# A transformer block on TensorE: the big SBUF buffers moved to other addresses

## The chip, the cores and the metric

The kernel runs on one core of one Trainium2 chip. The metric is the device time of one execution in microseconds, here the median of three runs.

## What is computed

One layer of a hybrid block on 256 tokens with 16 meta tokens ahead of them (272 in all), of width 2048, in float32: a feed-forward block, a mixer (windowed pooling beside latent attention, gated and projected), and a second feed-forward block, each with a norm before and after.

```python
def _swiglu(h, w_gu, w_down):
    g, u = jnp.split(h @ w_gu, 2, axis=-1)
    return (jax.nn.silu(g) * u) @ w_down

def _hybrid_mixer(h, w_in, ...):
    z = h @ w_in
    u_pool, c_q, c_kv, k_rope, g_pool, g_mla = jnp.split(z, SPLITS, axis=-1)
    y_pool = _multiscale_pool(u_pool, pool_w, pool_scale) @ w_pool_o
    y_mla = _mla(c_q, c_kv, k_rope, q_a_norm, w_q_b, kv_a_norm, w_kv_b, cos, sin) @ w_mla_o
    y = jax.nn.sigmoid(g_pool) * y_pool + jax.nn.sigmoid(g_mla) * y_mla
    return y @ w_out

h = h + 0.5 * _rmsnorm(_swiglu(_rmsnorm(h, norm_ffn1_pre[i]), ffn1_w_gu[i], ffn1_w_down[i]), norm_ffn1_post[i])
m = _hybrid_mixer(_rmsnorm(h, norm_mix_pre[i]), ...)
h = h + _rmsnorm(m, norm_mix_post[i])
h = h + 0.5 * _rmsnorm(_swiglu(_rmsnorm(h, norm_ffn2_pre[i]), ffn2_w_gu[i], ffn2_w_down[i]), norm_ffn2_post[i])
return h[:, N_META:]
```

The feed-forward blocks are 5632 wide, the attention has 16 heads.

## The kernel before

All activations stay in SBUF, transposed: features on the 128 partitions, tokens along the row. The weights come as one long stream of 128x128 tiles in the order of their use. A chunk of 8 tiles is loaded by one DMA on SyncE's queue into one of five `raw` buffers (4096 bytes in each partition), well ahead of its use. Four tiles at a time are split into two parts of 12 bits, `hi` (ScalarE, L92) and `lo` (VectorE, L93), in the type fp32r; each has six buffers of 2048 bytes. A product is then the sum of high by high, high by low and low by high.

The activations that are multiplied are split in the same way by the class `Two`, which keeps the high and the low part of a tile side by side. The weights' tile is always the stationary operand, the tokens are the moving one. There are two ways to issue the product with one tile of weights:

- `mm3` (L213 to L215), the narrow way: three matmuls, of 272 columns where all tokens take part and of 256 where the meta tokens don't. The first and the second load the high part of the weights, the third the low part. Their moving operands are the high, the low and again the high part of the tokens.
- `mm_wide` (L219 and L221): one matmul of 512 columns, the high part of the weights by both parts of 256 tokens, and one of 256 columns, the low part by the high one.

The first feed-forward and the first part of the mixer's `w_in` (up to about 920 us) are narrow with 272 columns. The gates (the rest of `w_in`, about 930 to 1115 us) are wide, but their moving operand `x` is laid out for 272 tokens, so that the 256 tokens begin 64 bytes into each row of 1088 bytes. The attention (to about 1300 us) has short products of many kinds: q, k, v, scores, probabilities by values, and the pooled branch's output projection `po`. From then on everything is wide, with operands laid out for 256 tokens: `o` by `w_mla_o` (to about 1400 us), `y` by `w_out`, and `x` and `a` in the second feed-forward. There a tile of the moving operand takes 2048 bytes, high part and low part of 1024 each. In the layout for 272 tokens it takes 2176, 1088 each.

Nothing is issued by a planner: the order is the program's own, with small delays counted in tiles of weights (`later`). The pools of SBUF lie one behind the other in the order in which they are opened, each buffer rounded up to 32 bytes:

- `keep`: `gains` (448 bytes), `const` (1024: identity and ones), `eps` (8), `acc`, `rs` (1088 each) and `small` (64);
- `raw`: five buffers; `parts`: six of `hi`, then six of `lo`;
- `big`: nine slots of 17408 bytes (34 times 512). They hold the residual `h`, the moving operands `x`, `a`, `y`, `o`, `D`, `Y`, `CB`, and other large tensors (`t`, `zp`, `zm`, `U`, `MA`, `VP`), each in turn;
- `tmp`: six buffers of 1088 bytes for single tiles on their way from PSUM, and some small ones.

Of the kernel before, what the change touches and what calls it, by code (L numbers as in the profile page):

```python
# [9 lines left out]
F32 = mybir.dt.float32  # L10
# [4 lines left out]
P = 128  # L15
# [3 lines left out]
R = 256  # L19
# [8 lines left out]
CH, PT = 8, 4  # L28
# [12 lines left out]
class Nothing:  # L41
    """Stands in for the builder's objects while the order of the weights is collected."""

# [16 lines left out]
class Weights:  # L60
    """The weights as one stream of [128, 128] tiles in the order of their use; each chunk of CH
    tiles is loaded ahead, and split, PT tiles at a time, into two parts of 12 bits, which together
    are the float32."""

# [32 lines left out]
    def take(self, *tiles):  # L97
        """The next tiles of the stream, side by side."""
        n = len(tiles)
        room = PT - len(self.order) % PT  # L100
        if room < n:
            self.order += [None] * room
        at = len(self.order)
        self.order += tiles
        if self.plan is None:
            return Nothing(), Nothing()
        assert self.plan[at : at + n] == list(tiles)
        p, j = divmod(at, PT)
        self.load((p + HL - 1) * PT // CH + RAW)
        self.divide(p + min(HL - 1, p // 2 + 2))  # L110
        for _ in tiles:
            self.tick()
        hi, lo = self.split[p]
        s = slice(j * P, (j + n) * P)
        return hi[:, s], lo[:, s]


class Later:
    """Work that is issued some steps of the weights' stream later, so that an engine isn't held
    by what another one has yet to do."""  # L120

# [3 lines left out]
    def __call__(self, *steps):  # L125
        """steps: pairs of a delay after the one before, and what to run then."""
        at = self.now
        for delay, run in steps:
            at += delay
            self.due.append((at, run))  # L130
        self.due.sort(key=lambda d: d[0])
# [11 lines left out]
def build(nc, tc, ctx, hT, wsrc, gains_d, const_d, tables_d, out, order):  # L143
# [6 lines left out]
    raw = ctx.enter_context(tc.tile_pool(name="raw", bufs=RAW))  # L150
    parts = ctx.enter_context(tc.tile_pool(name="parts", bufs=HL))
    big = ctx.enter_context(tc.tile_pool(name="big", bufs=9))
    tmp = ctx.enter_context(tc.tile_pool(name="tmp", bufs=6))
    psum = ctx.enter_context(tc.tile_pool(name="psum", bufs=8, space=bass.MemoryType.PSUM))

    later = Later()
# [14 lines left out]

# [1 line left out]
    h = slot3(KD, L, F32, "h")  # L173
# [9 lines left out]
    ident, ones = const[:, :P], const[:, P:]  # L183
    eps = keep.tile([P, 2], F32, tag="eps", name="eps")
    pool_e.memset(eps[:, 0:1], EPS)
    pool_e.memset(eps[:, 1:2], 4 * EPS)
    acc = keep.tile([P, L], F32, tag="acc", name="acc")
    rs = keep.tile([P, L], F32, tag="rs", name="rs")
    small = keep.tile([P, 16], F32, tag="small", name="small")

# [3 lines left out]
    class Two:  # L194
        """n tiles of T tokens in two parts of 12 bits, side by side."""

# [20 lines left out]
    def mm_wide(b, w, x, k, first, last):  # L217
        """The same with the product of the low part of x in columns of its own, from R on."""
        mm(b.rearrange("p (b c) -> p b c", b=2), w[0], x.both(k, R), start=first, stop=last,  # L219
           skip_group_check=True)  # L220
        mm(b[:, :R], w[1], x.hi(k, R), start=False, stop=last, skip_group_check=True)  # L221

    def join(b, s):
        """s: the sum of both halves of b, in two steps."""
        act(s, b[:, R:], AF.Copy)
        return GAP, lambda: dve.tensor_tensor(s, b[:, :R], s, op=ALU.add)

    def warm(n, x=ident):
        """Keeps the tensor engine's clock up while it has to wait."""
        b = bank("warm")  # L230
        for _ in range(n):
            mm(b[:, :P], x[:, :P], x[:, :P], start=True, stop=True)

# [1 line left out]
    def rms_sums(sources, T, n, half=False):  # L235
        """1 / sqrt(mean + eps), or half of it, of the tokens whose squares' sums over the
        partitions of `sources` add up to n * mean; the tokens are on partitions."""
        b = bank("rms")
        tt = (0, P, L - P)[: 3 if T == L else 2]
        m, c0 = len(tt), 400  # L240
        for i, s in enumerate(sources):
            for j, t0 in enumerate(tt):
                mm(b[:, c0 + j : c0 + j + 1], s[:, t0 : t0 + P], ones[:, :1],
                   start=i == 0 and j == 0, stop=i == len(sources) - 1, skip_group_check=True)
        sd = tmp.tile([P, 4], F32, tag="sd", name="sd", bufs=2)
        f = 4 if half else 1
        act(sd[:, :m], b[:, c0 : c0 + m], AF.Sqrt, scale=f / n, bias=eps[:, f // 4 : f // 4 + 1])
        dve.reciprocal(sd[:, :m], sd[:, :m])
        return b, sd

    def rms_spread(b, sd, T):
        """The same for all partitions, in the bank's first T columns."""
        for j, (t0, c) in enumerate(((0, 0), (P, 0), (L - P, P - NMETA))[: 3 if T == L else 2]):
            mm(b[:, t0 + c : t0 + P], sd[:, j : j + 1].to_broadcast([P, P]), ident[:, c:],
               start=True, stop=True)
# [8 lines left out]
    def squares(src, T, j, last=False):  # L264
        """Adds the squares of src to acc; the last ones stay apart, for `rms` to add."""
        if j == 0:
            act(acc[:, :T], src, AF.Square)
            return []
        s = temp("sq")
        act(s[:, :T], src, AF.Square)  # L270
        if last:
            return [s]
        pool_e.tensor_tensor(acc[:, :T], acc[:, :T], s[:, :T], op=ALU.add)  # L273
        return []
# [3 lines left out]

# [1 line left out]
    class Stream:  # L280
        """The residual stream's parts for the next products; `update` brings a tile of it up to
        date. Issued in stages that lead the products by a tile."""

# [18 lines left out]
        def scale(self):  # L302
            """The pre-norm's scales; products of the unscaled input are scaled by them."""
            b, sd = rms_sums([acc] + self.last, self.T, DM)
# [6 lines left out]
    def products(names, n_k, x, T, wave, evac, stream=None, hooks={}, narrow=()):  # L311
        """Tiles of x @ w, transposed: the first `wave` of them side by side, then one by one."""
        wide = [T == R and i not in narrow for i in range(len(names))]
# [32 lines left out]

# [1 line left out]
    def post(names, n_k, x, T, g_post, half, wave, wait):  # L348
# [26 lines left out]

# [1 line left out]
    def ffn(x, w_gu, w_down, g_post, wait):  # L377
# [27 lines left out]

    # ================= first feed-forward =================
    warm(10, zero)
# [8 lines left out]

    # ================= mixer =================
    x = advance(t, b, L, G_MPRE)
# [15 lines left out]
    def rotate(o, src, T):  # L434
        """Rotary embedding of rows [x1, x2, x1, x2] of 32 each; o may not be src."""
        c = slice(L - T, L)
# [33 lines left out]
    def windows(j):  # L470
        """Difference of the windows' means and the input, in parts."""
        w = WINDOWS[j // 2]
        s = u[:, j, :]
        n, i = 1, 0
# [17 lines left out]

    # columns of w_in in tiles: c_kv, k_rope twice, c_q, u_pool
    names = [("w_in", ("kv", j)) for j in range(4)] + [("w_in", ("kr", 0))]
# [57 lines left out]

# [1 line left out]
    o2 = Two(HEADS, R, "o")  # L554
# [40 lines left out]
    def proj_v(g):  # L595
        """Rows of v of four heads: tokens 0.., tokens 128.., and those from 256 on, by the high
        part of the input in rows 64.. and by the low part in rows 80.. ."""
        bs = [bank(f"v{i}") for i in range(3)]
# [47 lines left out]
    def turn(i):  # L646
        """Transposes the probabilities: keys 128.. and keys 0.. of the two times 128 queries. Of
        the first 128 queries' keys from 128 on only 16 exist, the rows below are zero; the second
        ones' keys from 256 on go to rows 64.. and again to rows 80.. of the last columns."""
        b = bank("pt")  # L650
# [49 lines left out]

# [1 line left out]
    y = Two(KD, R, "y")  # L702
# [17 lines left out]

    # ================= second feed-forward =================
    t, b = ffn(advance(t, b, R, G_F2PRE), "ffn2_w_gu", "ffn2_w_down", G_F2POST, (0, 0))
# [15 lines left out]
def columns(name, m):  # L738
    """Columns of a weight that make its tile m."""
    a = np.arange(P)  # L740
# [71 lines left out]
```

## Time and profile before

| | us |
|---|---|
| median of three runs | 2245.56 (2245.35 to 2246.13) |
| profiled execution, from its first to its last instruction | 2257.5 |
| TensorE busy in it | 2234.3 |
| VectorE, ScalarE, GpSimd busy | 1362.2, 1142.5, 205.4 |

The span is that of one execution under the profiler; no other time of that execution is listed. It is 11.9 us longer than the median of the runs. In the profile, PE is TensorE's matmuls and PEld its weight loads, which overlap them; DVE is VectorE, ACT is ScalarE, POOL is GpSimd, SP is SyncE. A group of the profile reads: line, engine, operation, what it writes and reads, shapes, number; busy time and the mean length of one; idle time of the engine before them and what ended it. Matmuls are pipelined, so the length of a single one is longer than the distance from its start to the next one's start, and that distance is what a matmul costs.

### The profile page before, as it was taken

To read this page: it belongs to the slowest core of one execution; us is meant where nothing else is said; L and a number is where in the kernel's file an instruction comes from. 1 tells how busy PE (TensorE), PEld (TensorE's weight loads), DVE (VectorE), ACT (ScalarE), POOL (GpSimd) and SP (SyncE) were. 2 spreads that over 40 slices of the span, in tenths; PEclk is the share of its full clock that TensorE was granted. 3 is DMA by queue.
4 is the path that set the end of the run, shared out by engine and by line. 5 is a ranking of instruction groups with operands and counts; after the bars stand their busy time and mean duration, and the time that the engine had idled before them with its cause. 6 is when DMAs were issued, how large, how long until landed. Compare 5 with 4: busy or idle time off the path is not lost.

```text
span 2257.5 us, 39449 instructions
## 1 busy us (share of the span) xinstructions
PE 2234.3 (99%) x15040; PEld 2062.4 (91%) x15040; DVE 1362.2 (60%) x2456; ACT 1142.5 (51%) x2273; POOL 205.4 (9%) x229
## 2 busy tenths in 40 slices
PE   9999999999999999999999999999999999999997
PEld 9999999999999999988888888888888888888886
DVE  6555555555444477766666677577666666654554
ACT  6444444444444454555544555665555555554543
POOL 2000000000000053200121111150000000000001
PEclk9999999999999999999999999999999999999999
DMA  6555555555555545566533356545655555655553
GB/s 242 178 175 174 179 172 178 177 170 177 177 169 180 175 150 168 178 190 188 173 113 122 114 169 195 186 151 186 185 188 184 188 186 186 187 191 187 187 182 117
DMA packets 109311, 393.46 MB, mean 174 GB/s; under 512 B 12288, under 2 KB 13696, under 8 KB 109120
## 3 DMA queue, kind: packets, MB, share of 16 engines
q1 hardware_dynamic: 108576, 389.19, 53.7%
q8 instruction: 118, 1.93, 0.4%
q0 software_dynamic: 400, 1.61, 0.2%
q14 instruction: 73, 0.60, 0.1%
q10 hardware_dynamic: 144, 0.13, 0.0%
HBM read 388.78 MB, written 2.10 MB: 173 GB/s over the span
## 4 chain that ended last, share of the span: by engine, by line
PE 97%; DVE 2%; issue 1%; DMA 0%; ACT 0%; SPq 0%; ACTq 0%; DVEq 0%
PE m L219 29%; PE m L221 15%; PE m L213 13%; PE m L215 12%; PE m L214 12%; PE w L219 2%; PE w L214 1%; PE w L221 1%; PE w L215 1%; PE s L622 1%; PE w L213 1%; PE po L213 1%; PE po L215 1%; PE po L214 1%; PE s L621 1%
## 5 line engine op out<-in xcount | busy, mean ns | idle before, releaser
L93 DVE TENSOR_TENSOR lo<-raw,hi 128x512 fp32r<-128x512 f32 x1472 | 1042.9, 722 | 691.7 <-ACT hi L92 686.7
L92 ACT ACTIVATE hi<-raw 128x512 fp32r<-128x512 f32 x1472 | 882.5, 625 | 393.6 <-PE m L214 283.1
L219 PE MATMUL m<-x,hi 128*128 128x512 f32 x1824 | 643.3, 398 | 0.0
L221 PE MATMUL m<-x,lo 128*128 128x256 f32 x1824 | 513.0, 281 | 0.0
L213 PE MATMUL m<-x,hi 128*128 128x272 f32 (+1 forms) x1488 | 429.6, 289 | 0.0
L215 PE MATMUL m<-x,lo 128*128 128x272 f32 (+1 forms) x1488 | 429.2, 288 | 0.0
L214 PE MATMUL m<-x,hi 128*128 128x272 f32 (+1 forms) x1488 | 428.4, 288 | 0.0
L219 PEld LDWEIGHTS m<-x,hi 128*128 128x128 f32 x1824 | 342.9, 188 | 83.2
L221 PEld LDWEIGHTS m<-x,lo 128*128 128x128 f32 x1824 | 345.0, 189 | 0.0
L214 PEld LDWEIGHTS m<-x,hi 128*128 128x128 f32 x1488 | 282.9, 190 | 0.0
L213 PEld LDWEIGHTS m<-x,hi 128*128 128x128 f32 x1488 | 279.8, 188 | 0.0
L215 PEld LDWEIGHTS m<-x,lo 128*128 128x128 f32 x1488 | 279.7, 188 | 0.0
L219 PE MATMUL m<-a,hi 128*128 128x512 f32 x660 | 233.2, 399 | 0.0
L273 POOL TENSOR_TENSOR acc<-acc,sq 128x272 f32<-128x272 f32 (+1 forms) x88 | 83.4, 948 | 1532.8 <-ACT sq L270 1532.5
L215 PE MATMUL m<-a,lo 128*128 128x272 f32 (+1 forms) x748 | 215.7, 288 | 0.0
L213 PE MATMUL m<-a,hi 128*128 128x272 f32 (+1 forms) x748 | 215.7, 288 | 0.0
L214 PE MATMUL m<-a,hi 128*128 128x272 f32 (+1 forms) x748 | 215.3, 288 | 0.0
L221 PE MATMUL m<-a,lo 128*128 128x256 f32 x660 | 185.4, 281 | 0.0
L219 PEld LDWEIGHTS m<-a,hi 128*128 128x128 f32 x660 | 124.1, 188 | 31.1
L214 PEld LDWEIGHTS m<-a,hi 128*128 128x128 f32 x748 | 142.4, 190 | 0.0
L213 PEld LDWEIGHTS m<-a,hi 128*128 128x128 f32 x748 | 140.8, 188 | 0.0
L215 PEld LDWEIGHTS m<-a,lo 128*128 128x128 f32 x748 | 140.8, 188 | 0.0
(206 smaller groups left out, 2577.4 us busy)
## 6 DMA issues: line engine op xcount, KB each, us to landing
raw<-w SPq DMA_DIRECT2D x735, 512.0 KB, 3.5
h<-hT POOLq DMA_DIRECT2D x4, 272.0 KB, 5.7
out<-t SPq DMA_DIRECT2D x8, 128.0 KB, 1.9
out<-t SPq DMA_DIRECT2D x4, 256.0 KB, 2.1
h<-hT SPq DMA_DIRECT2D x1, 544.0 KB, 9.1
raw<-w SPq DMA_DIRECT2D x2, 256.0 KB, 3.5
MA<-tables POOLq DMA_DIRECT2D x1, 480.0 KB, 3.7
h<-hT SPq DMA_DIRECT2D x2, 136.0 KB, 2.9
```

The lines of the kernel that those rows point to most:

```text
L92: nc.scalar.activation(hi, t, AF.Copy)
L93: nc.vector.tensor_tensor(lo, t, hi.bitcast(F32), op=ALU.subtract)
L213: mm(o, wh, xh, start=first, stop=False)
L214: mm(o, wh, xl, start=False, stop=False)
L215: mm(o, wl, xh, start=False, stop=last)
L219: mm(b.rearrange("p (b c) -> p b c", b=2), w[0], x.both(k, R), start=first, stop=last, skip_group_check=True)
L221: mm(b[:, :R], w[1], x.hi(k, R), start=False, stop=last, skip_group_check=True)
L273: pool_e.tensor_tensor(acc[:, :T], acc[:, :T], s[:, :T], op=ALU.add)
L621: mm(b[:, c : c + n], q[:, t0 : t0 + P], k[:, :n], start=True, stop=False)
L622: mm(b[:, c : c + n], qp[hp : hp + 64, t0 : t0 + P], kpe[hp : hp + 64, :n], start=False, stop=True)
```

## The change

`eps` moves from `keep` to a pool of its own, `shift`, with one buffer of 64 bytes that lies between `parts` and `big`. `small` grows from 16 to 80 columns; nothing more is stored in it. With the two, the buffers that follow get other addresses in each partition:

| buffers | before | after | before, modulo 512 | after, modulo 512 |
|---|---|---|---|---|
| `acc`, `rs` | 18016, 19104 | 17984, 19072 | 96, 160 | 64, 128 |
| `raw` (five, every 4096) | 20256 | 20480 | 288 | 0 |
| `hi` (six, every 2048) | 40736 | 40960 | 288 | 0 |
| `lo` (six, every 2048) | 53024 | 53248 | 288 | 0 |
| nine slots of `big` (every 17408) | 65312 | 65600 | 288 | 64 |
| `tmp`, first of six (every 1088) | 221984 | 222272 | 288 | 64 |

Before, all of these are 32 past a multiple of 64; afterwards they are multiples of 64. The difference between a slot's address and that of a weight buffer grows by 64 bytes.

```diff
     parts = ctx.enter_context(tc.tile_pool(name="parts", bufs=HL))
+    shift = ctx.enter_context(tc.tile_pool(name="shift", bufs=1))
     big = ctx.enter_context(tc.tile_pool(name="big", bufs=9))
...
-    eps = keep.tile([P, 2], F32, tag="eps", name="eps")
+    eps = shift.tile([P, 16], F32, tag="eps", name="eps")
     pool_e.memset(eps[:, 0:1], EPS)
     pool_e.memset(eps[:, 1:2], 4 * EPS)
     acc = keep.tile([P, L], F32, tag="acc", name="acc")
     rs = keep.tile([P, L], F32, tag="rs", name="rs")
-    small = keep.tile([P, 16], F32, tag="small", name="small")
+    small = keep.tile([P, 80], F32, tag="small", name="small")
```

The rest of the diff takes out comments. The instructions of every engine and every queue, and their order, are the same before and after; the lines of the program stand one further down from the new pool on (L213 becomes L214, L219 becomes L220).

## The prediction

> **What bounds the kernel now.** I read the summary page first, then the chain of work that ended last, the costliest groups, the list of what TensorE waited for, a table by stretches of time, and last the single matmuls in order of time.
>
> ```profile
> span 2257.5 us, 39449 instructions
> PE 2234.3 (99%) x15040; PEld 2062.4 (91%) x15040; DVE 1362.2 (60%) x2456; ACT 1142.5 (51%) x2273; POOL 205.4 (9%) x229
> PEclk9999999999999999999999999999999999999999
> PE 97%; DVE 2%; issue 1%; DMA 0%; ACT 0%; SPq 0%; ACTq 0%; DVEq 0%
> ...
> L93 DVE TENSOR_TENSOR lo<-raw,hi 128x512 fp32r<-128x512 f32 x1472 | 1042.9, 722 | 691.7 <-ACT hi L92 686.7
> L92 ACT ACTIVATE hi<-raw 128x512 fp32r<-128x512 f32 x1472 | 882.5, 625 | 393.6 <-PE m L214 283.1
> L219 PE MATMUL m<-x,hi 128*128 128x512 f32 x1824 | 643.3, 398 | 0.0
> L221 PE MATMUL m<-x,lo 128*128 128x256 f32 x1824 | 513.0, 281 | 0.0
> L213 PE MATMUL m<-x,hi 128*128 128x272 f32 (+1 forms) x1488 | 429.6, 289 | 0.0
> ...
> L213 PE MATMUL m<-a,hi 128*128 128x272 f32 (+1 forms) x748 | 215.7, 288 | 0.0
> ```
>
> TensorE is busy for 2234.3 of 2257.5 us at the full granted clock, and the chain lies on it for 97%. Its matmuls show no idle time before them. VectorE and ScalarE wait: the first for ScalarE's high parts, the second for TensorE to free a buffer of weights. Nothing shortens this kernel but shorter matmuls, and every nanosecond per matmul tells 15040 times. What TensorE waited for is next to nothing; the largest entry of that list is
>
> ```profile
> PE w L219 <- DVE x L298: 3.6, 7, 0.7
> ```
>
> A busy TensorE is not one at its peak, so I look at how many matmuls go through in a stretch (columns: the stretch, its length, busy time of PE with the number of its matmuls, then weight loads, VectorE, ScalarE, GpSimd, granted clock, DMA share, GB/s).
>
> ```profile
> 300.00:400.00 100.00, 100.00 (x799) 100.00 (x798) 57.38 (x103) 47.57 (x84) 0.00 (x0) 1.00 0.54 174
> 1000.00:1080.00 80.00, 80.00 (x465) 70.33 (x465) 48.73 (x89) 42.82 (x89) 0.56 (x2) 1.00 0.60 189
> 1320.00:1400.00 80.00, 80.00 (x463) 70.61 (x462) 59.36 (x101) 42.71 (x89) 16.22 (x16) 1.00 0.56 183
> 1900.00:2000.00 100.00, 100.00 (x567) 86.71 (x566) 64.72 (x123) 52.69 (x109) 0.00 (x0) 1.00 0.58 180
> ```
>
> I take one off each count, since a stretch cuts a matmul at its edge. In 300 to 400 us (narrow products, three matmuls of 272 columns for each tile of weights, "a triple") a matmul takes 100/798 = 125.3 ns, a triple 376. In 1900 to 2000 (wide products, 512 and 256 columns, "a pair") a pair takes 100/283 = 353.4 ns. In 1320 to 1400 the same two instructions, with `o` as the moving operand, take 80/231 = 346.3 ns. In 1000 to 1080 (the gates) 18 of the matmuls are those of the pooled products, six on each of three lines (by the groups of that stretch,
>
> ```profile
> L215 PE MATMUL pool<-D,lo 128*128 128x256 f32 x6 | 1.7, 281 | 0.0
> ```
>
> ), about 2.1 us at a third of a pair each, so a pair takes (80 - 2.1)/223 = 349.3 ns. So the same work on TensorE costs up to 2% more or less by stage, with the clock the same and no waits.
>
> The single narrow matmuls show that this goes with position, too (start, length, line; L213 begins a triple):
>
> ```profile
> 300.34 0.29 PE L213 MATMUL m<-x,hi 128*128 128x272 f32 x1
> ...
> 300.72 0.29 PE L213 MATMUL m<-x,hi 128*128 128x272 f32 x1
> ...
> 301.09 0.29 PE L213 MATMUL m<-x,hi 128*128 128x272 f32 x1
> ...
> 301.48 0.28 PE L213 MATMUL m<-x,hi 128*128 128x272 f32 x1
> ...
> 301.85 0.29 PE L213 MATMUL m<-x,hi 128*128 128x272 f32 x1
> ...
> 302.23 0.28 PE L213 MATMUL m<-x,hi 128*128 128x272 f32 x1
> ```
>
> From start to start 0.38, 0.37, 0.39, 0.37, 0.38 us: every second triple is about 10 ns dearer. In the program's addresses one thing alternates so: tile k of a narrow moving operand lies 2176 bytes, which is 4 times 512 and 128 more, after tile k-1, while the weight tiles lie 512 bytes apart. So the distance between what streams and what is being loaded, taken modulo 256, takes two values in turn. (The weight tile's own place in its buffer alternates as well, so this is a strong hint and no proof.)
>
> **The change, part by part.**
>
> *The weights' stationary parts `hi`, `lo`, and `raw`, from 288 to 0 modulo 512; the slots from 288 to 64.* On the wide products whose moving operand is laid out for 256 tokens, the moving address less the weight's goes from 0 to 64 modulo 256 in every pair. The nearest rows are the gates': their operand is laid out for 272 tokens and read 64 bytes in, so this distance is 64 and 192 in turn (and the 512 columns are in two pieces). They take 349.3 against 353.4. I take this row, since half of its pairs have exactly the new distance: 353.4 - 349.3 = 4.1 ns less. The pairs concerned are those of the second feed-forward and the output projection:
>
> ```profile
> L219 PE MATMUL m<-x,hi 128*128 128x512 f32 x1824 | 643.3, 398 | 0.0
> L219 PE MATMUL m<-a,hi 128*128 128x512 f32 x660 | 233.2, 399 | 0.0
> L219 PE MATMUL m<-y,hi 128*128 128x512 f32 x144 | 50.9, 399 | 0.0
> ```
>
> The gates' 32 tiles of 16 steps are 512 of the 1824, so 1824 - 512 + 660 + 144 = 2116 remain, and the waves of six tiles that begin the second feed-forward and the output projection add 6 x 16 each: 2308. Times 4.1 ns: 9.5 us less. The gates themselves get the distances 128 and 0 in place of 64 and 192, and the `o` stage leaves its good pattern of 346.3: if both land at 351, that is 512 x 1.7 + 256 x 4.7 = 2.1 us more. Bounds: all pairs as `o` now (2308 x 7.1 = 16 us less), or all one such step of 7.1 ns dearer than now (16 us more).
>
> *The narrow triples.* Their distances are 0 or 128 for the high part and 64 or 192 for the low part now; afterwards it is the other way round. The same four values occur, so I cost this at nothing. Bounds: every triple like the cheap ones (370 against 376: 6 x 2236 = 13 us less, with 1488 + 748 triples from the groups) or like the dear ones (385: 20 us more).
>
> *The attention's short products* (q, k and the pooled output) have all three distances at 0 now and get 64:
>
> ```profile
> L213 PE MATMUL po<-Y,hi 128*128 128x256 f32 x120 | 35.1, 293 | 0.0
> ```
>
> At the pair's saving of 4.1 ns for two matmuls, 2 ns for each is 1.4 us less: the code has 16 heads with 8 + 4 + 2 tiles (a rope tile serves two heads), three matmuls each, 672. Bounds: the same up and down.
>
> *Starts at a multiple of 64.* Every fp32r operand of this kernel starts 32 bytes past a multiple of 64 now, and none will afterwards. No row shows a matmul of this type with an aligned start. I take 0, as in the rows that only change the distance; what it may bring at most is the first rival, and a loss from alignment alone nothing in the trace suggests.
>
> *The operands of the other engines move too.* The 1472 splits take 625 ns on ScalarE and 722 ns on VectorE for four weight tiles; TensorE takes 4 x 376 = 1504 ns for four tiles, or 4 x 353 = 1412. A tenth more or less on either stays hidden. If that cover went, TensorE would show waits for `hi` or `lo`. The same covers the landing of `raw` (DMA share 0.54 to 0.60, the next chunk is five buffers ahead).
>
> *`eps` in a pool of its own, `small` of 80 columns, comments taken out.* No instruction is added or moved on any engine or queue; `eps` is still set twice by GpSimd in the first microseconds. Nothing.
>
> Sum: -9.5 + 2.1 + 0 - 1.4 = -8.8 us: the span of 2257.5 becomes 2248.7. The profiled span is 11.9 us over the median of the runs (2245.56); with the same difference, 2236.8, 0.4% less. Under 0.2% a measurement of this kernel could hardly tell from no change.
>
> **What the Trainium skill would make of it.** Two of its rules speak to the excess. "TensorE: Matmul & The Clock Gate", section Back-to-back issue gap, gives an isolated matmul N/2.4 + 2.5 ns; an estimate by it for a pair is 215.8 + 109.2 = 325 ns. The trace's 353.4 is 28 ns above that, so by that page there is room for about 7%, whatever the cause. The same page (Step-by-step: what each phase is for) says that the weight load has a read port of its own and takes no read bandwidth from the running matmul, and "SBUF — State Buffer" (SBUF: two separate sides) that TensorE never waits for another reader. By that rule the distance of the two addresses cannot matter and the sum is 0; that is the second rival. The alternating triples speak against it.
>
> **The rivals.**
>
> *Faster by far: a start off a multiple of 64 costs each read a step.* Pairs differ by 353.4 - 346.3 = 7.1 ns between stages, so costs seem to come in steps of about 7 ns. If each matmul now pays one such step because it starts in the middle of something, aligned starts save it everywhere: three times 2236 narrow matmuls, two times 3076 wide ones (2308 + 512 + 256 of `o`) and 670 short ones are 13500, times 7.1 ns = 96 us, to 2150. For it: the saving would be uniform, and all rows have the same misaligned start, so nothing excludes it. Against it: the gates read two pieces for their 512 columns, each with such a start, and are no dearer than the one piece of the others.
>
> *No change: the distance does not matter.* Then the alternation is the weight's place in its buffer, which stays, and the stages differ for another reason. `o` speaks for it: it has the distance 0 like `x` and `a` and yet takes 346.3. Time 2245.6.
>
> *Slower: the new distance locks into a dearer pattern.* The `o` stage shows that equal distances can settle at two prices. If the wide pairs settle one step higher than now, 2308 x 7.1 = 16.5 us more, 2262. It decides as soon as the mean pair of the second feed-forward is over 353.4 + 4.5/2.308 = 355.3 ns. For it: 0 is not shown to be the worst distance; `o` at 0 is the best row of all. Against it: the gates hold both 64 and 192 and are below 353.4.
>
> **How the numbers follow.** Likeliest is the sum above, with 0.34 (faster by some 0.2 to 1%, own range 2226 to 2241). The large gain has 0.28 (2145 to 2226, since only part of the matmuls may gain), no change 0.14, slower 0.24 (up to 2280, if triples and pairs both go up). Faster is thus 0.62, same 0.14, slower 0.24. Leaving out the outer tenth on each side, the range is 2155 to 2262.
>
> **What the profile of the changed kernel would show.** The number of matmuls between 1900 and 2000 us would be 573 or so in place of 567 if the pairs go to 349; 590 if every matmul loses a step; 567 if nothing happens; 556 in the slower case. Between 300 and 400 us I expect 799 again (about 846 if every matmul loses a step). Waits of TensorE should stay at a few microseconds. I am wrong if the narrow triples move by more than 4 ns either way, since they are half the time and I cost them at nothing, or if the alternation from triple to triple is still there with all its 10 ns while the pairs have gone down, since then two causes would be at work.

## The result and the profile after

The changed kernel takes 2265.64 us (median of 5 runs, 2265.49 to 2266.18), the kernel before 2246.13 in the runs beside it. The ratio of the means is 1.0076 with an interval of 1.0049 to 1.0102: slower by 0.8%, where 0.4% faster was forecast. By the medians it is 19.5 us.

One thing has to be known to read these numbers. The kernel before has two times. Of 130 executions of it, timed beside the runs told of here on several chips, 93 took 2243.5 to 2246.7 us and 36 took 2257.0 to 2259.8; the granted clock is the same in both kinds (0.997 to 0.998). Three single slow executions of 3110 us and more, one of them of this kernel, are passed over in all ranges. The share of the dearer kind differs: 1 of 21 in one round of runs and 19 of 35 in another, where the median itself was 2257.1 us. The medians of the cheaper kind lie between 2244.1 and 2245.8 by round, so times of different rounds compare to about 2 us. All four profiles taken of it, the one in the prediction too, are of the dearer kind. The changed kernel has one time.

The summary of the changed kernel, then its group of narrow matmuls, then the four stretches (columns as before: stretch, length, PE busy with its matmuls, weight loads, VectorE, ScalarE, GpSimd, clock, DMA share, GB/s):

```profile
span 2264.4 us, 39449 instructions
PE 2242.0 (99%) x15040; PEld 2072.2 (92%) x15040; DVE 1362.7 (60%) x2456; ACT 1142.1 (50%) x2273; POOL 205.6 (9%) x229
PEclk9999999999999999999999999999999999999999
PE 96%; DVE 2%; issue 1%; DMA 0%; ACT 0%; SPq 0%; ACTq 0%
...
L214 PE MATMUL m<-x,hi 128*128 128x272 f32 (+1 forms) x1488 | 431.6, 290 | 0.0
```

```profile
300.00:400.00 100.00, 100.00 (x791) 100.00 (x791) 55.48 (x99) 46.85 (x82) 0.00 (x0) 1.00 0.52 177
1000.00:1080.00 80.00, 80.00 (x467) 70.57 (x466) 49.92 (x92) 42.36 (x90) 0.56 (x2) 1.00 0.58 186
1320.00:1400.00 80.00, 80.00 (x455) 69.78 (x454) 59.59 (x101) 40.82 (x87) 16.40 (x15) 1.00 0.54 185
1900.00:2000.00 100.00, 100.00 (x568) 87.12 (x567) 65.59 (x125) 50.54 (x105) 0.00 (x0) 1.00 0.57 186
```

Nothing waits that did not wait before; TensorE is simply busy for 7.7 us longer. In the narrow stretch 791 matmuls go through in place of 799, in the `o` stretch 455 in place of 463, in the second feed-forward 568, the same to one matmul. The narrow part can be read sharply from starts of first matmuls that lie 24 triples apart (start, length, line), first in the changed kernel, then in a second profile of the kernel before:

```profile
300.33 0.29 PE L214 MATMUL m<-x,hi 128*128 128x272 f32 x1
...
309.45 0.29 PE L214 MATMUL m<-x,hi 128*128 128x272 f32 x1
```

```profile
300.19 0.29 PE L213 MATMUL m<-x,hi 128*128 128x272 f32 x1
...
309.23 0.29 PE L213 MATMUL m<-x,hi 128*128 128x272 f32 x1
```

That is 9.12/24 = 380.0 ns against 9.04/24 = 376.7 ns for a triple. The two products of the first feed-forward have 1312 + 704 triples after their first wave: 3.3 x 2016 = 6.7 us more. The narrow triples of `w_in` did not change (from 820 to 900 us 622 matmuls go through, 621 before). The `o` pairs go from 346.3 to 80/227 = 352.4 ns: 6.1 x 256 = 1.6 us more. The short products became cheaper, as in the groups of the pooled output, 36.2 us before and 35.7 now for the same 128 matmuls:

```profile
L216 PE MATMUL po<-Y,lo 128*128 128x256 f32 x128 | 35.7, 279 | 0.0
```

```profile
L215 PE MATMUL po<-Y,lo 128*128 128x256 f32 x128 | 36.2, 283 | 0.0
```

By the starts of the first matmuls of each stage, the whole attention takes 1.2 us less and every other stage is within 0.3 us. Profile to profile the change costs 2264.4 - 2257.5 = 6.9 us. The other 13 us of the medians are between the two times of the kernel before. So there were two questions: why the triples now take 380 ns, and where the 13 us lie.

### The profile page after: what moved, and what is told of

Its sections match the earlier page's. It is cut to its first block, busy times and chain, and to the rows that moved or that the text cites. A ratio compares the mean times of both kernels' runs of the same rounds, so it can differ in the third digit from the quotient of the medians.

```text
span 2264.4 us, 39449 instructions
## 1 busy us (share of the span) xinstructions
PE 2242.0 (99%) x15040; PEld 2072.2 (92%) x15040; DVE 1362.7 (60%) x2456; ACT 1142.1 (50%) x2273; POOL 205.6 (9%) x229
## 4 chain that ended last, share of the span: by engine, by line
PE 96%; DVE 2%; issue 1%; DMA 0%; ACT 0%; SPq 0%; ACTq 0%
PE m L220 29%; PE m L222 15%; PE m L214 13%; PE m L215 13%; PE m L216 12%; PE w L220 2%; PE w L215 1%; PE w L216 1%; PE w L222 1%; PE s L623 1%; PE w L214 1%; PE po L215 1%; PE po L214 1%; PE po L216 1%; PE s L622 1%
## 5 line engine op out<-in xcount | busy, mean ns | idle before, releaser
L220 PE MATMUL m<-x,hi 128*128 128x512 f32 x1824 | 643.2, 395 | 0.0
L214 PE MATMUL m<-x,hi 128*128 128x272 f32 (+1 forms) x1488 | 431.6, 290 | 0.0
L220 PEld LDWEIGHTS m<-x,hi 128*128 128x128 f32 x1824 | 342.5, 188 | 81.2
L214 PEld LDWEIGHTS m<-x,hi 128*128 128x128 f32 x1488 | 279.4, 188 | 0.0
L220 PE MATMUL m<-a,hi 128*128 128x512 f32 x660 | 233.2, 396 | 0.0
L214 PE MATMUL m<-a,hi 128*128 128x272 f32 (+1 forms) x748 | 216.5, 289 | 0.0
L220 PEld LDWEIGHTS m<-a,hi 128*128 128x128 f32 x660 | 124.0, 188 | 30.2
L214 PEld LDWEIGHTS m<-a,hi 128*128 128x128 f32 x748 | 140.4, 188 | 0.0
```

The lines of the kernel that those rows point to most:

```text
L214: mm(o, wh, xh, start=first, stop=False)
```

## Experiments

Two theories were set against each other. By the address theory the addresses of moving operand and weights set what a matmul costs. By the pattern theory the sequence of matmuls settles into one of several regular patterns, and addresses only set which patterns there are. 18 further kernels were run, three of them the kernel before again; times are medians.

**A second profile of the kernel before** (no edit).

> The kernel before, unchanged, for a second profile of it. The one on hand has a span of 2257.5 us, but its runs have 2245.4 to 2246.4 and one 2258.5; in the changed kernel span and time differ by under 2 us. So the profile of before may be of an execution that was 13 us dearer than most. Pattern theory (an execution settles in one of several regular patterns of matmul starts): the new profile spans some 2244 us, and one stage with the same addresses has another mean pair or triple than in the first profile; 13 us over the 2308 wide pairs of the second feed-forward and the output projection would be 5.6 ns a pair, so a pair of 347 to 350 ns in place of 353.4. Theory of a fixed offset (span is always 12 us over the time): 353.4 again, and 376 for the triples.

Measured: 2246.2 us; of 12 runs 8 took 2245.5 to 2246.5 and 4 took 2259.2 to 2260.6. The profiled one took 2259.2 with a span of 2257.4. So a span is under 2 us short of its own time, and the offset of 11.9 us that the prediction carried along was the difference between two kinds of execution. Two more profiles were taken:

> The kernel before once more, unchanged, for one profile. Its runs have two times, about 2246 and about 2259 us; the profiles on hand are all of the dearer one (span 2257.4). Pattern theory: a profile of a 2246 execution (span 2244) has the same instructions and no waits more or less, but one long stage with another mean: either narrow triples of about 370.7 ns in place of 376.7 (13.2 us over 2220 triples) or wide pairs of 347.6 in place of 353.3 (13.2 us over 2308 pairs). Rival: the 13 us are a single stop somewhere (a late transfer, a gap before a matmul), and all means are as before.

> As the run before it; with two, the chance to see the cheaper execution is better than with one. Same expectations.

Both were of the dearer kind again (2259.4 and 2259.0 us). No profile shows the cheaper execution. Where 36 of 129 executions are dear, four of four profiles by chance would be under 1%; it may be the profiled execution that is dear more often, which was not tested.

**The parts of the change, one by one.** Alignment alone (`small` of 72 columns, `eps` where it was), shift alone (`small` of 24, with the pool `shift`), and everything moved by 32 bytes (`small` of 24, `eps` where it was):

```diff
-    small = keep.tile([P, 16], F32, tag="small", name="small")
+    small = keep.tile([P, 72], F32, tag="small", name="small")
```

> One part alone: raw, hi, lo and the nine slots all at 0 modulo 512, so that moving operand and weights keep the distance of before (0) and starts are multiples of 64. Distance theory (the slower time comes from the 64 bytes between slots and weights): as before, 2245.6 us, narrow triple 376.6 ns. Alignment theory (multiples of 64 do it): as the changed kernel, 2265.6 us, narrow triple 380 ns. If executions settle by accident in either: between, and spread over more than 5 us.

> The other part alone: weights at 288 modulo 512 as before, the nine slots 64 further, at 352. Distance theory: as the changed kernel, 2265.6 us, narrow triple 380 ns, wide pair 353.3 ns. Alignment theory: as before, 2245.6 us, triple 376.6 ns.

> All buffers from raw on moved by 32 bytes, to 320 modulo 512: starts become multiples of 64 but not of 512, distance 0 as before. Distance theory: 2245.6 us. Alignment to 64: 2265.6 us. Alignment to 512 alone: 2245.6 us here and 2265.6 us in the kernel with all at 0.

Measured: alignment alone has the two times of the kernel before, 4 runs at 2245.3 to 2246.3 and 8 at 2258.8 to 2259.2, with triples at 376.7 ns and as many matmuls in its narrow stretch as before (columns from here on: stretch, length, PE busy with its matmuls, clock, DMA share, GB/s):

```profile
300.00:400.00 100.00, 100.00 (x799) 1.00 0.52 173
```

The move by 32 bytes gave 2258.4 to 2259.7 in 6 runs, the dearer of the same two. In both profiles every stage takes what it took before, to 0.3 us, so starts at multiples of 64 or 512 change no price by themselves. Their medians are 13 us higher all the same, since 14 of these 18 executions were of the dearer kind, against 10 of 41 of the kernel before on the same chip. Whether the addresses set that share was not settled: it varies by round for the kernel before, too. The shift alone takes 2254.5 us (2253.7 to 2254.9) in all 12 runs, and its triples are cheaper than any so far:

```profile
300.20 0.29 PE L214 MATMUL m<-x,hi 128*128 128x272 f32 x1
...
309.19 0.29 PE L214 MATMUL m<-x,hi 128*128 128x272 f32 x1
```

8.99/24 = 374.6 ns (374.4 to 374.5 over the whole products). Moving operands and weights are 64 bytes apart as in the changed kernel, which takes 380.0. The address theory had 380 here, the alignment theory 376.6: the distance matters, but by itself it does not set the price.

**The same addresses from another start.** In the changed kernel and in the kernel before, a useless small matmul stands ahead of each of the 16 output tiles of the first down projection, to knock the sequence out of step:

```diff
             b = bank("m")
+            # ahead of this, in products(), for the first down projection only
+            mm(bank("warm")[:, : 8 * i + 8], ident, const[:, : 8 * i + 8], start=True, stop=True)
             for k in range(n_k):
                 part(i, k, b)
```

> The changed kernel with one small float32 matmul of 8, 16, ... 128 columns (of the identity, its result unused) ahead of each of the 16 output tiles of the first feed-forward's down projection, which knocks the regular sequence out of step in 16 different ways. Pattern theory: with the same addresses, triples of the down projection settle in patterns other than 380 ns in some tiles (374.4 as in the kernel with the shift alone, or 376.7), so their mean over 704 triples is below 380 and the kernel may gain 2 to 4 us although it does more. Address theory (the addresses alone set the price): each tile goes back to 380 ns after a few triples, and the kernel is 2 to 8 us slower by the 16 small matmuls.

> The same small matmuls in the kernel before. Pattern theory: triples of the down projection take several different means by tile, 376.7 and others (near 370.7 if that is where its cheaper executions differ). Address theory: 376.7 in all tiles after a few triples, the kernel 2 to 8 us slower.

Measured in the changed kernel: 2267.8 us. The small matmuls themselves, in order of time, show the length of each tile of 44 triples between them:

```profile
544.63 0.28 PE L344 MATMUL warm<-const 128*128 128x8 f32 x2
```

```profile
561.34 0.29 PE L344 MATMUL warm<-const 128*128 128x16 f32 x2
```

```profile
578.28 0.30 PE L344 MATMUL warm<-const 128*128 128x24 f32 x2
```

```profile
594.98 0.30 PE L344 MATMUL warm<-const 128*128 128x32 f32 x2
```

```profile
611.92 0.31 PE L344 MATMUL warm<-const 128*128 128x40 f32 x2
```

16.71, 16.94, 16.70 and 16.94 us: tiles of the same work at the same distance differ by 0.235 us, or 5.3 ns for each of 44 triples. After the first few, the triples of a tile repeat to 1 ns or so: either two by two (378 and 382 ns, or 379 and 381), with a mean of 379.9 to 380.0, or six by six (375, 376, 380, 368, 374, 374), with a mean of 374.3. Five of the 16 tiles take the cheaper way. Without the small matmuls all 16 take 379.9 or 380.0, so it is not the tile, its buffers of weights or its place in PSUM. This is the pattern theory's sign, though the gain of 2 to 4 us that it allowed did not come: the kernel is 2.1 us slower. In the kernel before, all 16 tiles went back to 376.7, as the address theory had it: there only one narrow pattern was seen. Its runs still had two times, 2249.2 to 2249.6 and 2260.7 to 2264.1, so the 13 us most likely do not lie in the first down projection.

**Choosing the pattern.** Two such matmuls of 8 columns in the changed kernel, then four:

```diff
+            n = {("ffn1_w_gu", 6): 8, ("ffn1_w_down", 0): 8, ("ffn2_w_gu", 6): 16, ("ffn2_w_down", 0): 64}.get((names[0][0], i))
+            if n:
+                mm(bank("warm")[:, :n], ident, const[:, :n], start=True, stop=True)
             b = bank("m")
```

> The changed kernel with two small float32 matmuls of 8 columns: one ahead of the first of the tiles of the first gate-and-up projection that are made one by one, one ahead of the first tile of the first down projection. Pattern theory: as in the first tile of the run with 16 of them, the triples settle at 374.4 ns in place of 380 and stay there, through both products: 2200 x 5.56 = 12.2 us less, 2253.6 us. Address theory: 2265.8 us.

> The same, and one small matmul of 16 columns ahead of the first single tile of the second gate-and-up projection and one of 64 columns ahead of the second down projection, the places and sizes after which pairs of the changed kernel took 348.9 in place of 353.3 ns. Pattern theory: another 2000 x 4.4 = 8.9 us less, 2244.8 us, so that the changed addresses with four useless matmuls are level with the kernel before. Address theory: 2266 us. If the choice of a pattern can't be repeated from one program to the next: 2253 to 2266 us with 353.3 in the wide pairs.

Measured with two: 2258.7 us (2258.0 to 2258.9), 6.9 less than the changed kernel, though it does more. Its profile says why it is half of what was expected:

```profile
300.00:400.00 100.00, 100.00 (x803) 1.00 0.53 175
600.00:700.00 100.00, 100.00 (x792) 1.00 0.54 173
```

In the gate-and-up projection the triples are at 374.4 (803 matmuls in 100 us, as in the shift alone); in the down projection, after the second small matmul, they are at 380 again. 1312 triples times 5.56 ns are 7.3 us. With four: 2253.7 us (2253.0 to 2256.8), and the wide part does the same:

```profile
1700.00:1800.00 100.00, 100.00 (x575) 1.00 0.58 189
2100.00:2200.00 100.00, 100.00 (x568) 1.00 0.58 190
```

575 matmuls are pairs of 100/287 = 348.4 ns in the second gate-and-up projection, 568 the usual 353 in the down projection. So within one program, at fixed addresses, both prices stand beside each other, and four matmuls that compute nothing used bring back 11.9 us of time (12.5 us of span). What failed is the choice by rule: in both down projections the start led to the dear pattern. The small matmul of 8 columns ahead of the first down projection shows it: at the same place, of the same size and with the same addresses, it was followed by 374.3 ns where the triples before it took 380, and by 379.9 where they took 374.6. What a start leads to depends on what ran before it.

**The wide products.** Small matmuls ahead of wide tiles, in the kernel before and in the changed one (`w_out` and the second down projection at each tile, the second gate-and-up projection at every sixth):

> The kernel before with a small float32 matmul of 8 to 128 columns (result unused) ahead of output tiles of the wide products: all of w_out's and of the second down projection's, every sixth of the second gate-and-up projection's (14). Pattern theory (the 13 us between the two times of the kernel before lie in the wide products): in the profile the pairs between two small matmuls take 353.3 ns in some tiles and 346.7 (or some other value below) in others, with the same addresses, and the runs scatter over several values between 2246 and 2266. Rival (addresses alone, the 13 us lie elsewhere): 353.3 in every tile, and two times as before, each 4 to 12 us later.

> The same small matmuls in the changed kernel. Pattern theory in its strong form: its wide pairs, too, take other values than 353.3 in some tiles. In its weak form: at the distance of 64 there is only the one pattern of 353.3, so the kernel is 4 to 12 us slower than 2265.6 in all runs; that would be the reason why its runs have one time where the kernel before has two.

Measured: 2267.6 us and 2271.5 us, each with one time. In the kernel before all tiles of the profile stay at 353.3. In the changed kernel most do, and three of the stretches of six tiles in the gate-and-up projection and the second half of the down projection take 348.9. Below, two cheap stretches stand above two at 353.3; of the matmuls counted, two in the first line and four in the second are the small ones:

```profile
1543.00:1603.00 60.00, 60.00 (x347) 1.00 0.57 185
1640.00:1700.00 60.00, 60.00 (x344) 1.00 0.59 186
```

With small matmuls in the second down projection of the kernel before alone:

> The kernel before with small float32 matmuls ahead of the 15 wide output tiles of the second down projection only. Small matmuls ahead of tiles of w_out and of both second products left one time (2267), those in the first down projection left two, 12 to 14 us apart. If the 13 us lie in the wide products after w_out, and the small matmuls force the dearer pattern where they stand: two times that are 13.2 x 1408/2112 = 8.8 us apart, the cheaper one at 2246 + 4.4 + 2 to 4 us for the small matmuls = 2252 to 2254. If they lie in w_out or the attention: still 13 us apart. If they lie in the down projection alone: one time.

Measured: 4 runs at 2252.2 to 2253.5 and 8 at 2260.3 to 2262.4. The middles of the two are 8.2 us apart, where 8.8 was expected if the 13 us lie in both wide products of the second feed-forward (9.6 by the 14.5 us between the two times of the kernel before in the same round). And its profile, of a dearer execution, had `w_out` in another pattern than the other profiles at the distance 0, 175 matmuls in place of 172, though up to there it is the same program at the same addresses as the kernel before. That line stands first, the one of the kernel before second:

```profile
1430.00:1460.00 30.00, 30.00 (x175) 1.00 0.56 188
```

```profile
1430.00:1460.00 30.00, 30.00 (x172) 1.00 0.53 176
```

30/87 = 345 ns in place of 351 (346.6 and 353.4 by the starts over the single tiles): wide pairs at the distance 0 do have the cheaper pattern, not in the `o` stage only. In all these profiles the pairs of `w_out` begin at 346.7, as those of `o` before them; in the others they change to 353.3 after 17 pairs, in this one they don't. 13.2 us over the 2068 pairs of the second feed-forward are 6.4 ns each, about the 6.7 between the two. That these pairs are at 346.7 in the cheaper executions is inferred from the two runs; it was seen in no profile.

**Other distances.** Weights at 288 modulo 512 throughout; the pool `shift` sets the distance in the narrow products (8 columns for 32 bytes, 24 for 96, 16 for 64), and operands for 256 tokens start some columns into their slot:

```diff
-            self.s = [src or slot(self.at, F32R, f"{name}{i}") for i in range(-(-n // 8))]
+            off = 24 if T == R else 0
+            self.s = [src or slot(self.at + off, F32R, f"{name}{i}")[:, off:] for i in range(-(-n // 8))]
```

> Other distances between the moving operand and the weights (weights at 288 modulo 512 as before): 32 bytes in the narrow products, 128 in the wide ones. If the distances matter in steps of 64, the narrow triples are as with 0 or with 64 (376.7, 374.4 or 380). For the wide pairs the gates, which hold 128 and 0 in turn after the change, take 350: 349 to 352 expected, a time of 2240 to 2262 us. If a distance of 32 makes it worse in every triple: over 2270.

> The same with 96 bytes in the narrow products and 192 in the wide ones. The gates, which hold 64 and 192 in turn before the change, take 350: wide pairs of 349 to 352 expected; narrow triples of 374 to 380; a time of 2240 to 2262 us.

> Weights at 288 modulo 512 as before; moving operand and weights 64 bytes apart in the narrow products (as in the shift alone, 374.4 ns a triple) and 0 apart (modulo 256) in the wide ones, as before. Pattern theory: the narrow part gains 4.9 us (2.23 ns over 2200 triples) on the kernel before, and the wide part has the two patterns of before: 2241 and 2254 us, with more of one or of the other. Rival (one price for one pair of addresses): a single time, near 2246 - 4.9 = 2241 us.

Measured: with 32 and 128, 2260.3 us, triples of 380.0 and pairs of 351.1, as expected. With 96 and 192, 2256.2 us, triples of 375.0 and pairs of 353.3, where 349 to 352 were expected: the gates are no guide to the other wide products. With 64 and 0 (`off` of 48), 2254.7 us, triples of 374.4 and pairs of 353.3, `o` included, and one time in 12 runs, where both theories had 2241 for some or all of them:

```profile
1700.00:1800.00 100.00, 100.00 (x567) 1.00 0.57 185
```

At the distance 0 modulo 256, but elsewhere, the cheaper pattern of the wide products did not come up at all, which refutes the rule that the distance modulo 256 gives the patterns. Modulo 512 this distance is 256, while it is 0 in all the kernels that showed 346.7 or had two times; the rule that the distance modulo 512 gives the patterns that can come up fits all the runs, and nothing was run to test it.

**A version that beats both?** The shift alone, with one small matmul of 16 columns ahead of the second gate-and-up projection's single tiles, and with a second one ahead of the second down projection:

> The shift alone (weights at 288 modulo 512, slots at 352; 2254.5 us, triples 374.4, pairs 353.3) with one small float32 matmul of 16 columns ahead of the first single tile of the second gate-and-up projection, after which the changed kernel's pairs took 348.9 there. Pattern theory: 348.9 through that projection, 5.8 us less by 1312 pairs: 2248.8 us; if the pattern is kept in the down projection, too, 2246 us, the cheaper time of the kernel before and 13 us under its dearer one. If absolute addresses matter for which pattern follows a given start: 353.3 and 2254.8 us.

> The same with a second one of 16 columns ahead of the second down projection. Pattern theory: as the run before it in the gate-and-up projection; 348.9 in the down projection if the start after it is like that in the projection before (2246 us), 353.3 if not (2249 us).

Measured: 2254.8 us and 2252.1 us. The first did nothing. After the second the down projection took the cheaper pattern (100/287 = 348.4 ns), while the gate-and-up projection did not, the other way round than in the changed kernel:

```profile
1700.00:1800.00 100.00, 100.00 (x568) 1.00 0.57 186
2100.00:2200.00 100.00, 100.00 (x575) 1.00 0.57 191
```

No version was found that is below the cheaper time of the kernel before.

## Why the prediction was wrong

Of the 19.5 us, about 13 are a wrong base, and 6.9 were measured, profile to profile, where -8.8 were forecast.

*The base.* The first failed step is "The profiled span is 11.9 us over the median of the runs (2245.56); with the same difference, 2236.8". The profile was of an execution of about 2259 us; in the changed kernel the span is 1.8 us below its own time. The price of the second feed-forward read from it was the dearer of two, by what the runs let infer, and even the forecast gain of 8.8 us from about 2259 would have ended near 2250, above the median.

*The wide pairs.* The second failed step is "I take this row": 349.3 ns from the gates for the distance of 64. Measured 353.3, so the term of -9.5 us was 0. The row was a wrong neighbour: its operand is laid out otherwise, and by the starts of their pairs the gates take 350.0 ns (the 349.3 was a rough count) in all 20 profiles, whatever the distance. So the row never held a price of the distance, and the gates stayed at 350 where 351 was forecast. From 1900 to 2000 us 573 matmuls were forecast and 568 came. What I had seen and passed over was in the same fence: `o` at 346.3 and `x` at 353.4 with the same distance could not both be a price of the distance.

*The narrow triples.* The third is "I cost this at nothing": measured 3.3 ns more each in the first feed-forward, 6.7 us, inside the bound of 20 that stood beside it. The reason given, that the same four values only change places, took each distance to have its price. By the starts in the traces, triples of about 372 and 381 ns took turns before and triples of 378 and 382 do now: the prices did not change places. With the shift alone, where the distances change in the same way, the mean is 2.2 ns less. The prediction's own sign of being wrong here, 4 ns either way, was set too wide to catch it.

*The `o` stage and the short products.* Forecast +1.2 us and -1.4 us. The two parts of +2.1 were 0.9 for the gates, measured 0, and 1.2 for `o`, measured 1.6. The three lines of `po` alone give -1.3 (37.4 + 36.2 + 36.2 against 37.0 + 35.8 + 35.7 us), the whole attention -1.2. Right in size, and small. The 672 matmuls of that term are those of q and the pooled output; k, named beside them, is laid out for 272 tokens and isn't among them.

*The rivals.* The large gain by aligned starts is refuted: alignment alone has the two times of the kernel before. No change is refuted by the result. The slower rival had the mechanism, "locks into a dearer pattern", which had 0.24; its place was wrong. Pairs were to go a step above 353.4 and did not. It was the triples that rose, and, as far as the runs let infer, the second feed-forward that no longer reached its cheaper pattern.

*The Trainium skill.* The prediction estimated 325 ns for a pair by the formula for an isolated matmul in the Trainium skill, "TensorE: Matmul & The Clock Gate" (Back-to-back issue gap), and called the 28 ns above it room for about 7% (28 of 353.4 are 8%). No profile has a product whose pairs take less than 346.6 ns on the mean, so nothing here shows that room. The same page of the Trainium skill (Step-by-step: what each phase is for) says that the weight load takes no read bandwidth from the running matmul, from which the prediction reasoned that no distance could matter. With alignment alone the triples stay at 376.7, with the shift alone they go to 374.4 in all profiles that have its narrow addresses. The measurement decides: in this kernel the distance has an effect, though what waits for what was not seen.

*What stays open.* What in the chip makes the patterns, what decides from one execution to the next between the two times of the kernel before, and why its profiles were all of the dearer kind, was not settled. That the changed kernel never reaches the cheaper kind is what its runs show; why is open.

## What to carry to other kernels

Before costing a change of a percent, compare the span of the profile with the time of its own execution and with the other runs: several microseconds between them say that the profile is of another kind of execution than the median. A kernel bound by back-to-back matmuls can settle, product by product, into patterns that differ by 1 to 2% at the same addresses; counting matmuls per 100 us shows them. A gain or loss of that size from moving buffers, or from any edit that shifts the start of a product, can then be the choice of a pattern and need not survive the next edit.

## What the runs showed of the hardware

- Means of triples in the first feed-forward took few sharp values, 374.4, 375.0, 376.7 and 380.0 ns, and those of pairs with operands laid out for 256 tokens 346.7, 348.9, 351.1 and 353.3. Each held for long stretches, mostly whole products, and changed near the beginning of a product (in `w_out` after 17 pairs) or after a small matmul.
- At one set of addresses two prices were seen in one program: 374.4 and 380.0 for triples, 348.9 and 353.3 for pairs (the changed kernel's addresses), and 346.7 and 353.3 for pairs (the addresses of before). The same product, `w_out`, took either in two executions of the same addresses.
- A small matmul of 16 columns, placed once ahead of it, was followed by 348.9 in place of 353.3 ns through a product of 1312 pairs in one kernel (1.2%) and did nothing at the same place in another.
- The pairs of the gates took 350.0 ns in all 20 profiles, at several distances.
